# A streaming encoder layer on one core: where a head gain is multiplied, and the order of three short stages

## The chip, the cores and the metric

The kernel runs on one core of one Trainium2 chip. The metric is the device time of one execution in microseconds (us), given as the median of several runs. The engines are TensorE (PE, with its weight loads shown apart as PEld), VectorE (DVE), ScalarE (ACT), GpSimd (POOL) and SyncE (SP, which here only issues transfers). Each engine takes its instructions in a fixed order, and a waiting instruction holds all that stand behind it on its engine.

## The reference

One layer of a hybrid encoder, for 1024 new tokens and 32 tokens of a running stream (the decode tokens). All of it is in f32.

```python
def mixer(xn, ...):                       # xn = rms_norm(x, g_mix_pre)
    proj = xn @ w_in                      # split into q, k, v, gates of three head groups
    o_a = head_rms_norm(gla(...), g_a) * silu(gr)
    o_b = head_rms_norm(hgrn2(...), g_b) * silu(hg)
    o_c = head_rms_norm(mlstm(...), g_c) * sigmoid(mo)
    cat = concatenate([o_a, o_b, o_c], axis=-1)
    return cat @ w_out                    # g_a, g_b, g_c together are g_head, one number per column of cat

x = x + rms_norm(mixer(...), g_mix_post)
up = causal_dwconv(rms_norm(x, g_ffn_pre) @ w_up)
gate, val = split(up)
x = x + rms_norm((gelu(gate) * val) @ w_down, g_ffn_post)
```

`head_rms_norm(x, g)` divides each head by its root mean square and multiplies by g. So g_head is one factor per column of `cat`, and may as well be one factor per row of `w_out`.

## The kernel before, in words

**Arithmetic.** Most products are made from two halves of each f32 operand: a high half rounded by a cast (`xh`, `woh`, ...) and a low half, the difference (`xl`, `wol`, ...). A product is then three matmuls, high by high, low by high and high by low (`mm3`, lines 87 to 90), which accumulate in one bank of PSUM. `split` (line 92) makes the halves: ACT casts, DVE subtracts.

**Stages.** The tokens are cut into three groups (384, 384, and 256 with the 32 decode tokens). For each group the input projection runs (`inproj`): first the token-major v columns and gates (`vg`, tiles `pv`, one block `blk` of 256 columns after another, one tile for every 128 tokens), then the feature-major q, k and forget columns (tiles `pf`). The third group makes its v and gate blocks feature-major and turns them back (`vg_across`, tiles `pv`, `vf`, `pb`). The work of the mixer in units of 128 tokens (units 0 to 7, and 8 for the decode tokens; `mixer`) is interleaved with the projections of the following groups, until some 487 us. Then the output projection of the units follows (`outproj`; the first is `RING[0]`, unit 0), interleaved with the mixers of units 6 and 7, until some 641 us. The seam to the up-projection runs from there to some 675 us, then the up-projection `up_all` until after 1200 us, and `down_all` to the end. The up-projection forms each 2 x 2 block of products by seven products p1 to p7 of sums of blocks (`PROD`; operands A.. and S.. of the weights, B.. and T.. of the tokens), and `s` is 0 or 1 for the two halves of 256 tokens that the first step takes apart.

**What sets the order.** The program writes generators that hand over to each other with `yield`, and a scheduler orders the instructions of every engine by their priorities and its own estimates; `tc.high_priority` moves instructions forward, `tc.issue_after` keeps them behind a given one. So a small edit can move instructions far from it. Tiles come from pools; a tag with `bufs=n` has n places in turn, and who writes a place waits for the readers of the tile that lay there before.

**The places that matter here:**
- Gates. `vg_store` takes a bank `pv` or `pb`. Blocks 4 to 7 are gates: ACT makes a tanh into `vth` (or `gth` in the third group), DVE completes it (L432, L434), POOL multiplies by `gh`, the broadcast half of g_head, into `vg` (L436), and POOL issues the write to the DRAM tensor `g_d` (L437). The mixer reads it back as `gt` and multiplies it into `cat`.
- Keys. `keys` transposes a unit's four key blocks on PE into the bank `mi`, two at a time. ACT copies both halves of each pair into `kt2` (64 x 256, L888); the second pair goes into the same bank.
- First out-projection unit. `out_weights` makes `woh` and `wol` from the raw tiles `wor`, six of which are loaded early. The ring of 128 x 1024 tiles has `NRING` = 7 places, and `CT0` = 6 raw tiles lie ahead of the first `ct` tile; the last two raw tiles follow later. `outproj` transposes `cat` (tiles `ct`, `ctp`, halves `ch`, `cl`) and makes for every k both halves of the columns, three matmuls each. `om` and `cat` of the decode unit, 8, stand among them.
- Seam. `up_block` for f = 0 and s = 0, 1, with the operands of f = 1 being made meanwhile by `up_operands`, and the T2 and T4 operands copied on ACT (L2047).

## Time and profile before

| | |
|---|---|
| median of 3 runs | 1328.7 us (1328.49 to 1329.58) |
| profiled execution | 1326.9 us, its span 1325.1 us, mean granted PE clock 0.992 |
| PE busy | 1290.7 us, 97% of the span |
| DVE busy | 1008.1 us, 76% |
| ACT busy | 700.0 us, 53% |
| POOL busy | 286.1 us, 22% |
| chain of work that ended last | PE 73%, DVE 14%, DMA 4%, ACT 4%, issue 3%, POOL 2% |

The span is the time between the first and the last instruction in the profile; 1.8 us of the execution lie around it. A row of a timeline has the start in us from the span's beginning, the duration of the row, engine, line, operation, output and inputs, shapes, and the number of instructions that it joins; in brackets stands the idle time of the engine before it and what ended it. Tile names are written without numbers, so `kt` is the program's `kt2`, and `q` or `fr` stand for tiles of any group. Matmuls overlap, so a row's duration is not its share of PE's time. The granted clock of PE is 1.00 at full rate.

### The profile page before, as it was taken

What the parts mean: (1) busy time and instruction counts of PE and PEld (TensorE: products, weight loads), DVE (VectorE), ACT (ScalarE), POOL (GpSimd) and SP (SyncE); (2) the same over time, 40 slices, a digit from 0 to 9 for tenths busy, and PEclk for the clock granted to TensorE, in tenths of its full rate; (3) what the DMA queues carried; (4) which work ended last, traced back from release to release, by engine and by line L of the source; (5) the groups of instructions that cost most, each with busy time, mean ns of one, the idle gap of its engine ahead of it and who ended that gap; (6) DMA issues with size and microseconds to landing.
All of it is one profiled execution on the core that took longest, in us unless ns stands there. A gap on an engine that the chain in (4) does not pass through costs nothing.

```text
span 1325.1 us, 25585 instructions
## 1 busy us (share of the span) xinstructions
PE 1290.7 (97%) x9896; PEld 1095.0 (83%) x9896; DVE 1008.1 (76%) x1761; ACT 700.0 (53%) x1298; POOL 286.1 (22%) x390
## 2 busy tenths in 40 slices
PE   6999999999989999999999999999999999999997
PEld 6999889998889987868887777778888887778885
DVE  5795639778698778786997777778888876499556
ACT  5655556555575555445864545445455454454552
POOL 4532403145122263223100101111111000020005
PEclk9999999999999989999999999999999999999999
DMA  9799778886889954634439988855574349845425
GB/s 340 244 356 372 263 254 253 301 275 198 301 277 306 348 173 151 192 110 150 132 147 306 299 245 246 243 154 152 136 182 129 100 148 353 327 141 152 136 88 127
DMA packets 134784, 291.73 MB, mean 220 GB/s; under 512 B 29015, under 2 KB 63991, under 8 KB 132535
## 3 DMA queue, kind: packets, MB, share of 16 engines
q1 hardware_dynamic: 119831, 262.71, 58.4%
q0 software_dynamic: 10320, 22.94, 8.7%
q10 hardware_dynamic: 4512, 4.46, 1.0%
q8 instruction: 77, 1.26, 0.4%
q14 instruction: 44, 0.36, 0.1%
HBM read 229.38 MB, written 85.78 MB: 238 GB/s over the span
## 4 chain that ended last, share of the span: by engine, by line
PE 73%; DVE 14%; DMA 4%; ACT 4%; issue 3%; POOL 2%; SPq 0%; DVEq 0%; POOLq 0%; ACTq 0%
PE pux_None L88 4%; PE pux_None L90 4%; PE pux_None L89 4%; PE puw_None L90 3%; PE puw_None L88 3%; PE puw_None L89 3%; PE q L88 3%; PE q L90 3%; PE q L89 3%; PE pv L88 3%; PE pv L89 2%; PE pv L90 2%; PE x L88 2%; PE x L89 2%; PE x L90 2%
## 5 line engine op out<-in xcount | busy, mean ns | idle before, releaser
L1453 DVE SCALAR_TENSOR_TENSOR y<-uu,fconv_sb,y 128x1024 f32<-128x1024 f32 x88 | 112.9, 1283 | 21.8 <-ACT y L1451 20.1
L1450 POOL COPY fhalo<-uu 128x2 f32<-128x2 f32 x44 | 18.3, 416 | 382.5 <-DVE uu L1363 382.5
L1451 ACT ACTIVATE y<-uu,fconv_sb 128x1024 f32<-128x1024 f32 x44 | 54.8, 1245 | 5.6 <-DVE uu L1363 5.1
L88 PE MATMUL pv<-wt_0h,xh_all 128*128 128x256 f32 (+1 forms) x192 | 56.1, 292 | 0.9 <-DVE xl_all L326 0.7
L89 PE MATMUL zp<-wol,ch 128*128 128x512 f32 (+1 forms) x144 | 57.0, 396 | 0.0
L88 PE MATMUL zp<-woh,ch 128*128 128x512 f32 (+1 forms) x144 | 57.0, 405 | 0.0
L90 PE MATMUL zp<-woh,cl 128*128 128x512 f32 (+1 forms) x144 | 56.6, 394 | 0.0
L90 PE MATMUL pv<-wt_0h,xl_all 128*128 128x256 f32 (+1 forms) x192 | 54.7, 285 | 0.0
L89 PE MATMUL pv<-wt_0l,xh_all 128*128 128x256 f32 (+1 forms) x192 | 54.6, 284 | 0.0
L88 PE MATMUL pv<-wt_1h,xh_all 128*128 128x256 f32 (+1 forms) x192 | 54.3, 283 | 0.0
L89 PE MATMUL pv<-wt_1l,xh_all 128*128 128x256 f32 (+1 forms) x192 | 54.3, 283 | 0.0
L90 PE MATMUL pv<-wt_1h,xl_all 128*128 128x256 f32 (+1 forms) x192 | 54.3, 283 | 0.0
L211 POOL TENSOR_SCALAR gss<-gss 128x1 f32<-128x1 f32 (+1 forms) x9 | 13.0, 1442 | 175.2 <-ACT gjk L1722 175.1
L206 POOL TENSOR_SCALAR hrs<-hss 128x5 f32<-128x5 f32 (+3 forms) x27 | 10.7, 396 | 171.1 <-DVE hss L1011 166.5
L827 DVE COPY_PREDICATED P<-masks_sb,sc 128x352 f32<-128x352 int32 (+3 forms) x53 | 38.0, 716 | 7.9 <-PE sc L738 7.3
L88 PEld LDWEIGHTS pv<-wt_0h,xh_all 128*128 128x128 f32 x192 | 36.4, 190 | 2.2 <-DVE xl_all L326 1.1
L1011 DVE TENSOR_REDUCE hss<-sq 128x5 f32<-128x320 f32 (+3 forms) x27 | 13.6, 504 | 30.9 <-ACT sq L1010 30.8
L89 PEld LDWEIGHTS pv<-wt_0l,xh_all 128*128 128x128 f32 x192 | 36.4, 190 | 0.1
L90 PEld LDWEIGHTS pv<-wt_0h,xl_all 128*128 128x128 f32 x192 | 36.4, 189 | 0.1
L207 POOL TENSOR_TENSOR hrs<-hrs,mhalf 128x5 f32<-128x5 f32 (+3 forms) x27 | 35.9, 1329 | 2.2
L88 PEld LDWEIGHTS pv<-wt_1h,xh_all 128*128 128x128 f32 x192 | 36.0, 187 | 0.3 <-issue 0.2
L89 PEld LDWEIGHTS pv<-wt_1l,xh_all 128*128 128x128 f32 x192 | 35.9, 187 | 0.1
(1900 smaller groups left out, 4632.4 us busy)
## 6 DMA issues: line engine op xcount, KB each, us to landing
wus<-in_w_us SPq DMA_DIRECT2D x16, 1024.0 KB, 10.1
wrP<-in_w_dn SPq DMA_DIRECT2D x27, 512.0 KB, 8.5
ht<-h_d SPq DMA_DIRECT2D x22, 512.0 KB, 8.3
wt_0r<-in_w_tok SPq DMA_DIRECT2D x21, 512.0 KB, 3.8
wt_1r<-in_w_tok SPq DMA_DIRECT2D x21, 512.0 KB, 7.3
h_d<-y SPq DMA_DIRECT2D x21, 512.0 KB, 2.6
ws_d<-in_w_dn POOLq DMA_DIRECT2D x20, 512.0 KB, 7.8
wrP<-ws_d SPq DMA_DIRECT2D x20, 512.0 KB, 6.2
```

The costliest lines, as they stand in the source:

```text
L88: pe.matmul(ps, lh[0], rh[0], start=first, stop=False, **kw)
L89: pe.matmul(ps, lh[0], rh[1], start=False, stop=False, **kw)
L90: return pe.matmul(ps, lh[1], rh[0], start=False, stop=last, **kw)
L206: pool.tensor_scalar(out, ss, 1.0 / width, eps, op0=ALU.mult, op1=ALU.add)
L207: pool.tensor_tensor(out, out, mhalf[:n, :cols], op=ALU.pow)
L211: pool.tensor_scalar(out, m0, m1, EPS, op0=ALU.add, op1=ALU.add)
L827: dve.copy_predicated(dst, mk.broadcast_to([n, 11, *mk.shape[2:]]), src)
L1011: dve.tensor_reduce(ss[:n, h0:h0 + nh], sq3, axis=mybir.AxisListType.X, op=ALU.add)
L1450: behind["POOL"] = pool.tensor_copy(fhalo[:, j, :], u[:, SEQ - 2:SEQ])
L1451: act.activation(y, u, AF.Identity, scale=fconv[:, j, 2:3], bias=fconv[:, j, 3:4])
L1453: dve.scalar_tensor_tensor(y, uu[i][:, s:s + SEQ], fconv[:, j, s:s + 1], y, op0=ALU.mult, op1=ALU.add)
```

## The change

- **g_head.** POOL's product L436, the tile `gh`, its load and its scaling go. `gcols` gets eight columns more, g_head by rows of `w_out` (`ghead`, halved once on DVE). `out_weights` multiplies: the high half is an ACT activation with `ghead` as its scale, the low half a DVE scalar_tensor_tensor (raw times `ghead`, less the high half). The tanh goes straight into the tile that is written to `g_d`; the tag `vg` has four places instead of three, and `vth` is gone. In the third group the tile written to `g_d` is the `gth` tile itself.
- **Keys.** All four transposes go into the bank in one visit, and ACT then makes two copies of 64 x 512 instead of four of 64 x 256.
- **First out-projection unit.** `NRING` is 10 and `CT0` 8, so that all raw tiles are loaded ahead of the first `ct`. The unit first makes the products with the high weights for all k (four matmuls for each k), then those with the low weights. All low halves are kept behind `halves[1]`, the `cl` of the unit.
- **vf.** The copies of `vf` are issued at high priority.
- **Seam.** p7 of f = 0, s = 0 is kept behind the latest product; the A12 operand of f = 1 is made a step earlier, and the copies of T4 stand behind it; p3 of s = 1 stands behind p4.

The core of the diff:

```diff
         def vg_store(blk, u, off, n, ps):
-            o = mx.tile([128, 256], F32, tag="vg", name=f"vg{u}_{blk}", bufs=3)
             t = t0 + off
+            o = gate[0].tile([128, 256], F32, tag="gth", name=f"gth{u}_{blk}", bufs=3) if gate and blk > 3 else \
+                mx.tile([128, 256], F32, tag="vg", name=f"vg{u}_{blk}", bufs=4)
...
-            ia = tanh(th[:n], ps[:n, :256], 0.5)
+            ia = tanh(o[:n], ps[:n, :256], 0.5)
...
-            pool.tensor_tensor(o[:n], th[:n], gh[:n, c0:c0 + 256], op=ALU.mult)
             pool.dma_start(g_d[t:t + n, c0:c0 + 256], o[:n])
...
-                    act.copy(fs[e], ps)
+                    with tc.high_priority(offset=AHEAD):
+                        act.copy(fs[e], ps)
...
-    NRING, CT0 = 7, 6
+    NRING, CT0 = 10, 8
...
         def keys():
-            for f0 in (0, 2):
-                kps = small(2, 128)
-                for f in (f0, f0 + 1):
-                    soon(pe.transpose, kps[:n, f - f0, :], khf[:, f * n:f * n + n], ident)
-                for ch, (o, m) in enumerate(chunks):
-                    with tc.high_priority(offset=AHEAD):
-                        act.copy(kt2[o:o + m, ch, 128 * f0:128 * f0 + 256], kps[o:o + m].rearrange("p f n -> p (f n)"))
+            kps = mi.rearrange("p a b -> p (a b)").rearrange("p (f n) -> p f n", n=128)
+            for f in range(4):
+                soon(pe.transpose, kps[:n, f, :], khf[:, f * n:f * n + n], ident)
+            for ch, (o, m) in enumerate(chunks):
+                with tc.high_priority(offset=AHEAD):
+                    act.copy(kt2[o:o + m, ch, :], kps[o:o + m].rearrange("p f n -> p (f n)"))
...
     def out_weights(W):
         for k in range(8):
-            if k < 2:
-                split(W[1][k], W[2][k], wo_raw[k], dve)
-            else:
-
-                with tc.issue_after(halves[0].ins):
-                    act.copy(W[1][k], wo_raw[k])
-                with tc.issue_after(halves[1].ins):
-                    dve.tensor_tensor(W[2][k], wo_raw[k], W[1][k].bitcast(F32), op=ALU.subtract)
+            with tc.issue_after(halves[0].ins) if k > 1 else ExitStack():
+                act.activation(W[1][k], wo_raw[k], AF.Copy, scale=ghead[:, k:k + 1])
+            with tc.issue_after(halves[1].ins):
+                dve.scalar_tensor_tensor(W[2][k], wo_raw[k], ghead[:, k:k + 1], W[1][k].bitcast(F32), op0=ALU.mult,
+                                         op1=ALU.subtract)
             yield
...
                 next(W[3])
+                for x in range(2):
+                    for hf in range(2):
+                        pe.matmul(pss[hf][:n], chs[k][x], woh[k][:, cs[hf]], start=k + x == 0, stop=False,
+                                  skip_group_check=True)
+            for k in range(8):
                 for hf in range(2):
-                    product(pss[hf], hf, k)
+                    pe.matmul(pss[hf][:n], chs[k][0], wol[k][:, cs[hf]], start=False, stop=k == 7, skip_group_check=True)
...
         def prod(ps, p, first, last):
-            product(ps, p, W, X, first, last, at)
+            with tc.issue_after(ends[-1]) if f == 0 and p == "p7" else ExitStack():
+                product(ps, p, W, X, first, last, at)
...
-            with tc.issue_after(kept["B11"].ins):
-                for n in ("T2", "T4"):
+            for n, ins in (("T2", "B11"), ("T4", "A12")):
+                with tc.issue_after(kept[ins].ins):
                     for t, e in zip(X[n], early[n]):
                         act.copy(t[:, :, :256], e)
```

Where the scheduler puts things now is read from the order of the instructions of the two programs. The numbers behind names tell tiles apart and differ between the programs.

PE at the keys of unit 4 (`mi<-ident,kh` are the transposes of its keys, `rows` a small stage of the third group's gates, `pf_10` and `pf_11` two feature blocks of the projection). Before, the second pair stands between them:

```order
L90 MATMUL pf_10_5380<-xh_all,wf_10l 128x288
L629 MATMUL rows_5433<-r_dc_5010,cf_sb 128x5 x3
L631 MATMUL rows_5433<-ident,r_st_4999 128x128 x2
L631 MATMUL rows_5433<-ident,r_st_4999 32x128
L738 MATMUL mi<-ident,kh_5161 128x128 x2
L88 MATMUL pf_11_5451<-xh_all,wf_11h 128x288
```
Now all four transposes stand ahead of `pf_10`, and here is:

```order
L90 MATMUL pf_10_5320<-xh_all,wf_10l 128x288
L627 MATMUL rows_5373<-r_dc_4952,cf_sb 128x5 x3
L629 MATMUL rows_5373<-ident,r_st_4941 128x128 x2
L629 MATMUL rows_5373<-ident,r_st_4941 32x128
L88 MATMUL pf_11_5391<-xh_all,wf_11h 128x288
```
The key transposes are gone from behind `rows`, and `pf_11` follows at once.

DVE at the same place (`q<-th,pf_1` empties the bank that `pf_11` needs; `Qz`, `Ld` and `x` belong to unit 4's scores, `e` and `fr` to the third group's forget gates). Before:

```order
L861 TENSOR_TENSOR Qz_152<-x_2_5493,qe_5305 128x128 x2
L549 TENSOR_TENSOR e_4703<-e_4703 128x288
L847 TENSOR_TENSOR x_8_5660<-b_5137 128x512
L852 TENSOR_TENSOR Ld_150<-x_2_5493,k_5136 128x128x2
L857 TENSOR_TENSOR Qz_152<-x_2_5493,q_5135 128x128
L548 TENSOR_SCALAR fr_4702<-fr_4702,oml 128x288
L553 SCALAR_TENSOR_TENSOR e_4703<-cf_sb,e_4703 128x288
L567 SCALAR_TENSOR_TENSOR q_5285<-th_5287,pf_1_5260 64x288
```
Now:

```order
L854 TENSOR_TENSOR Qz_153<-x_2_5433,qe_5247 128x128
L565 SCALAR_TENSOR_TENSOR q_5227<-th_5229,pf_1_5202 64x288
L542 SCALAR_TENSOR_TENSOR e_4645<-fr_4644,e_4645 128x288
L854 TENSOR_TENSOR Qz_153<-x_2_5433,qe_5247 128x128
L547 TENSOR_TENSOR e_4645<-e_4645 128x288
L845 TENSOR_TENSOR Ld_151<-x_2_5433,k_5078 128x128x2
L850 TENSOR_TENSOR Qz_153<-x_2_5433,q_5077 128x128
L840 TENSOR_TENSOR x_8_5600<-b_5079 128x512
```
q has moved ahead of one Qz and of the rows e, Ld, Qz and x, which now follow it.

DVE at the first out-projection unit (`wol` is the last low half, `cl` the low half of the next unit's transposed `cat`, `cat` the decode unit's own, which reads the bank `og` that PE's `om` takes next). Before:

```order
L1073 TENSOR_TENSOR wol_6902<-wor_6871,woh_6894 128x1024
L942 TENSOR_TENSOR C_0_7760<-C_1_6507,dcs_5434 128x195
L804 TENSOR_TENSOR kh_7404<-b_7349 128x512
L847 TENSOR_TENSOR x_32_7420<-b_7349 128x512
L1011 TENSOR_REDUCE hss_7052<-sq_6_7273 32x5
L792 COPY dec_7396<-eb_7394 128x8
L798 TENSOR_TENSOR qz<-q_7347,eb_7394 32x2x128 x2
L798 TENSOR_TENSOR qz<-q_7347,eb_7394 32x128 x2
L798 TENSOR_TENSOR qz<-q_7347,eb_7394 64x256
L798 TENSOR_TENSOR qz<-q_7347,eb_7394 64x384
L1102 TENSOR_TENSOR cl_7040<-ctp_7034,ch_7039 128x512
L1013 TENSOR_TENSOR cat_7051<-og_7201,hrs_7053 32x384
```
Now, from the rows behind that low half on, and again at its end:

```order
L1091 TENSOR_TENSOR cl_6954<-ctp_6948,ch_6953 128x512
L1003 TENSOR_REDUCE hss_6966<-sq_0_7179 32x6
L935 TENSOR_TENSOR C_0_7143<-C_0_7143,mi 128x130
L936 TENSOR_TENSOR C_0_7143<-C_0_7143,mi 64x65
L797 TENSOR_TENSOR kh_7317<-b_7262 128x512
```
```order
L791 TENSOR_TENSOR qz<-q_7260,eb_7307 64x384
L800 TENSOR_TENSOR kh_7317<-kh_7317,k_7261 128x512
L1005 TENSOR_TENSOR cat_6965<-og_7114,hrs_6967 32x384
L934 TENSOR_TENSOR C_0_7671<-C_1_6447,dcs_5374 128x195
L845 TENSOR_TENSOR Ld_151<-x_32_7333,k_7261 128x8x32
```
`cl` has moved to the front, directly behind the low halves; the C product (`C<-C,dcs`) has moved behind `cat`, and the product of `kh` with k ahead of it.

More of the change, by code (lines that the diff above doesn't have):

```diff
@@ L239, in small @@
         return t if len(shape) == 1 else t.rearrange("p (a b) -> p a b", b=shape[1])
-    gh = p1.tile([128, 1024], F32, name="gh")
     cols_of, dcs_of, behind = {}, {}, {}
@@ L493, in vg_across @@
             load_cat(0)
-            for k in range(CT0, 8):
-                wo_raw.append(ring[0](f"wor{k}"))
-                raw_out(k)
         tgs = pf.tile([128, 3, 26], F32, tag="tgs", name=f"tgs{g}")
@@ L1309, in up_operands @@
         yield res
-        with tc.high_priority(offset=AHEAD) if f == 1 else ExitStack():
-            for name, src in (("A12", a12), ("A11", a11)):
+        for name, src in (("A12", a12), ("A11", a11)):
+            with tc.high_priority(offset=AHEAD) if f == 1 else ExitStack():
                 res[name] = weight_halves(f"{name}_{f}h", src)
+            if f == 1 and name == "A12":
+                yield
         with tc.issue_after(kept["T2l"].ins) if f == 1 else ExitStack():
@@ L1432, in up_block @@
             prod(z, "p4", True, True)
+            if s:
+                with tc.issue_after(ends[-1]):
+                    prod(w, "p3", False, True)
         out(0, 1, c6, w)
@@ L1541, in up_all @@
                     next(late, None)
+                    if f == 0:
+                        ops = up_operands(1, raw.pop(1))
+                        W[1] = next(ops)
+                        next(ops)
+                        yield
                     m = (2 * f + (1 if s is None else s) - 3) * len(SUMS) // 34
@@ L1554, in up_all @@
                 if s != 0 and f + 1 < NF:
-                    ops = up_operands(f + 1, raw.pop(f + 1))
-                    W[f + 1] = next(ops)
+                    if f:
+                        ops = up_operands(f + 1, raw.pop(f + 1))
+                        W[f + 1] = next(ops)
                     for _ in ops:
@@ L2048, in body @@
             for x, c in zip(last, (slice(0, 128), slice(128, 256))):
-                with tc.issue_after(done[0].ins), tc.issue_after(kept["c6"].ins):
+                with tc.issue_after(kept["first"].ins), tc.issue_after(kept["c6"].ins):
                     next(x)
```

28 lines of the change are left out of this document (15 added, 13 removed).

## The prediction

> **What bounds the kernel now.** I read the busy times of the page first, then TensorE's (PE's) waits, then stretches cut around the longest of them.
>
> ```profile
> PE 1290.7 (97%) x9896; PEld 1095.0 (83%) x9896; DVE 1008.1 (76%) x1761; ACT 700.0 (53%) x1298; POOL 286.1 (22%) x390
> ```
> ```profile
> PE xt L322 <- DVE x L302: 9.6, 1, 9.6
> PE mi L738 <- ACT kt L888: 5.2, 2, 3.1
> ```
> ```profile
> PE pv L88 <- ACT vf L486: 1.5, 3, 1.2
> PE oi L738 <- DVE cat L1013: 1.1, 1, 1.1
> ```
> PE is busy 1290.7 of 1325.1 us, so 34.4 us are idle (a wait's columns: us in total, times, longest). The first 9.6 us are the start, which the change leaves alone, as it does the end. It can win only among the small waits between, and in what the clock does after them. The columns of the next rows are the length, the busy time of PE, PEld, DVE, ACT and POOL, then PE's granted clock:
>
> ```profile
> 139.60:145.50 5.90, 3.21 (x98) 2.45 (x98) 5.76 (x17) 4.41 (x12) 1.67 (x3) 1.00 0.64 235
> 145.50:148.90 3.40, 3.40 (x23) 2.95 (x24) 3.18 (x9) 1.98 (x6) 2.13 (x3) 0.50 0.51 143
> 391.20:394.70 3.50, 0.40 (x3) 0.20 (x2) 3.47 (x11) 3.15 (x9) 0.00 (x0) 1.00 1.07 360
> 394.70:398.10 3.40, 3.09 (x13) 3.04 (x13) 3.34 (x8) 3.34 (x12) 0.58 (x2) 0.50 0.95 296
> 656.90:660.90 4.00, 1.79 (x6) 0.89 (x6) 4.00 (x8) 3.86 (x9) 0.00 (x0) 1.00 0.00 0
> 660.90:664.30 3.40, 3.40 (x9) 2.63 (x8) 3.40 (x6) 0.00 (x0) 0.00 (x0) 0.51 0.00 0
> 700.00:750.00 50.00, 50.00 (x248) 37.28 (x241) 38.01 (x50) 22.23 (x33) 3.95 (x6) 1.00 0.93 296
> ```
> Three times a stretch in which PE idles 2.7, 3.1 and 2.2 us is followed by 3.4 us at a clock of 0.50. Half of 3.4 is 1.7 us of PE work lost each time, where PE is the bound. From 700 us on PE is busy 50.00 of 50 us: what is won before arrives at the end undiminished. But in the second and third pair DVE is busy 3.47 of 3.50 and 4.00 of 4.00 us. There PE's wait is the visible side of a full DVE.
>
> The Trainium skill (TensorE: Matmul & The Clock Gate, its table of what to keep to) asks for no idle gap over about 3 us between matmuls; by that, stretches with 2.2 to 2.7 us of idle would keep the clock. The rows show that they did not, so the trace decides, and I charge 1.7 us from about 2 us of idle on. By the skill's rule alone the sum below would be 2.6 us larger.
>
> **The change part by part.** *Keys of unit 0.* The second pair of transposes waits for the copies of the first pair, which lie in the same bank: one of the two waits for kt, 5.2 - 3.1 = 2.1 us.
>
> ```profile
> 141.37 0.66 PE L322 MATMUL xt<-ident,x 128*128 128x128 f32 x4 [0.38 <-DVE vth L432]
> ```
> ```profile
> 141.43 0.43 ACT L856 ACTIVATE x<-x 128x256 f32<-128x256 f32 x1
> ```
> ```profile
> 141.57 0.87 POOL L436 TENSOR_TENSOR vg<-vth,gh 128x256 f32<-128x256 f32 x1 [2.20 <-ACT x L850]
> ```
> ```profile
> 141.56 1.03 DVE L861 TENSOR_TENSOR Qz<-x,qe 128x128 f32<-128x128 f32 x2
> ```
> ```profile
> 142.72 0.48 DVE L861 TENSOR_TENSOR Qz<-x,qe 128x128 f32<-128x128 f32 x2
> ```
> Four transposes in one visit leave this wait no place, and the new order puts whole projections behind the keys. What goes: 5.90 - 3.21 = 2.69 us of idle, and 1.7 us of clock. What is late next: the first of these projections needs a bank that a tanh empties, and on ACT that tanh stands behind the exponential that now ends at 141.86. With a tanh of some 0.4 us (rows below) it ends near 142.3 to 142.5. Until then, from 139.6 on, PE has only eight transposes, 2 x 0.66 us: 2.8 - 1.3 = 1.5 us idle, in pieces. So 2.69 - 1.5 = 1.2 us are won if the clock still falls, 2.9 if it doesn't, 4.4 if no wait is left. I take **2.9**: the pieces are nearest to the single wait of 1.2 us for vf above, which no half clock follows.
>
> The gate product leaves POOL (36 of about 0.87 us). POOL is on no path here; but the two DVE products beside it took 1.03 us and the next two 0.48, so each costs DVE 0.55 us. The Trainium skill (SBUF — State Buffer, Who interferes with whom) says that a DVE instruction with two SBUF inputs and a GpSimd one that reads SBUF contend; the rows agree.
>
> *Keys of unit 4.* The longest wait inside, 3.1 us until 394.34:
>
> ```profile
> 381.27 0.45 DVE L577 SCALAR_TENSOR_TENSOR r_fm<-r_fm,e 5x288 f32<-5x288 f32 x1 [1.70 <-ACT e L537]
> ```
> ```profile
> 384.68 0.49 DVE L1011 TENSOR_REDUCE hss<-sq 128x5 f32<-128x320 f32 x1 [0.84 <-ACT sq L1010]
> ```
> ```profile
> 405.12 0.46 DVE L546 TENSOR_TENSOR fr<-e,fr 64x288 f32<-64x288 f32 x1
> ```
> ```profile
> 407.35 0.95 DVE L827 COPY_PREDICATED P<-masks_sb,sc 128x352 f32<-128x352 int32 x1
> ```
> ```profile
> 408.89 0.75 PE L738 MATMUL sc<-Qz,Ld 64*64 64x64 f32 x36
> ```
> The wait goes, and q, for which the next projection waits, moves forward on DVE. PE would stand before the score matmuls of 408.89 up to 3.1 + 1.7 = 4.8 us earlier, at 404.1. But these need the masked copy that DVE ends at 408.30, and ahead of that copy DVE has the same work as before except the 0.46 us of fr. It can be earlier by that and by the 0.84 us that it stood for a reduction (now further behind), 1.3 us together, and at best by the 1.70 us as well. So PE goes on at 407.0, at best at 405.3: 1.9 or 3.6 us won. The rest of the old wait comes back as up to 2.9 us (407.0 - 404.1) for DVE; with a half clock behind it, where PE is the bound, 0.2 us is left. I take **1.0**, about halfway from 0.2 to 1.9, as the new wait falls in two or three pieces. The other seven units' keys have no such wait and win nothing.
>
> *First out-projection unit.* All raw weights are there early, the high halves go first, the low halves follow:
>
> ```profile
> 502.01 1.23 DVE L1073 TENSOR_TENSOR wol<-wor,woh 128x1024 fp32r<-128x1024 f32 x1 [0.50 <-ACT woh L1071]
> 504.94 0.36 DVE L942 TENSOR_TENSOR C<-C,dcs 128x195 f32<-128x195 f32 x1 [1.71 <-DMA out_q_c<-C]
> ```
> ```profile
> 509.96 0.53 DVE L1013 TENSOR_TENSOR cat<-og,hrs 32x384 f32<-32x384 f32 x1
> 510.43 0.67 DVE L807 TENSOR_TENSOR kh<-kh,k 128x512 f32<-128x512 f32 x1
> ```
> ```profile
> L1190 ACT ACTIVATE z<-xr,oss x8: 1136/1151/1156, 523.3 to 651.2; 128x1024 f32<-128x1024 f32 x8
> ```
> ```profile
> L1073 DVE TENSOR_TENSOR wol<-wor,woh x6: 1209/1218/1227, 495.0 to 502.0; 128x1024 fp32r<-128x1024 f32 x6
> ```
> ```profile
> L311 DVE SCALAR_TENSOR_TENSOR x<-x,rs,gx x8: 1273/1285/1759, 12.0 to 307.8; 128x1024 f32<-128x1024 f32 x7, 32x1024 f32<-32x1024 f32 x1
> ```
> A scaled high half costs ACT 1.15 us, a low half DVE 1.29 instead of 1.22: eight times 0.07 are 0.5 us. PE's products would end some 4 us earlier. Yet behind the transposes of the next unit stands the decode unit's om, and it waits for this cat. Ahead of cat DVE loses the waits of 1.71 (the C product moves behind) and 0.50 us and the C product itself, 0.36; it gains kh, 0.67, and the 0.5. So cat ends 1.71 + 0.50 + 0.36 - 0.67 - 0.5 = 1.4 us earlier, and PE waits for it about as much longer as its products end sooner than that, some 2.6 us. Ends: 1.4, and with a half clock behind that wait -0.3. I take **-0.3**, as all three long idles above were followed by one.
>
> *Casts of vf.* Put at high priority, but in ACT's order vf still stands behind squares that wait for DVE:
>
> ```profile
> 472.14 0.47 ACT L1010 ACTIVATE sq<-hn 128x320 f32<-128x320 f32 x1 [1.20 <-DVE hn L1041]
> ```
> Ends 0 and 1.2; **0.3**, for a DVE with no POOL products beside it. For the same reason the 1.1 us of oi, among the second group's gates: **0.4**, ends 0 and 1.1.
>
> *Seam.* p7 moves behind p2, the A12 cast ahead of the T4 copies. PE's 2.2 us at 656.9 go or move, but DVE is full:
>
> ```profile
> 651.00:675.00 24.00, 21.79 (x140) 19.28 (x139) 23.50 (x34) 17.84 (x27) 0.77 (x2) 0.93 0.17 9
> ```
> ```profile
> 667.33 1.22 DVE L1262 TENSOR_TENSOR T4l<-xg,T4h 128x1024 fp32r<-128x1024 f32 x1
> ```
> ```profile
> 670.09 0.28 PE L89 MATMUL puz<-T4l,A_0h 128*128 128x256 f32 x1
> ```
> DVE ends T4l at 668.55 behind the same work as before; PE uses it at 670.09. More than these 1.5 us can't be won. Ends -0.2 (less a half clock of 1.7) and 1.5; I take **1.0**, near the upper end, as the present half clock lies ahead of this point and is paid already.
>
> The rest (the gh load, its scaling, the merged key copies, the scaling of ghead) stands where PE waits for nothing: 0.
>
> Sum: 2.9 + 1.0 - 0.3 + 0.3 + 0.4 + 1.0 = 5.3 us. Lower ends: 1.2 + 0.2 - 0.3 + 0 + 0 - 0.2 = 0.9; upper: 4.4 + 3.6 + 1.4 + 1.2 + 1.1 + 1.5 = 13.2. The profiled execution took 1326.9 us (span 1325.1); the median, 1328.7, lies 1.8 above it. So 1321.6 on the profiled execution, **1323.4** on the median.
>
> **The rivals.** *Waits only change their name.* DVE is full at two of the three places, and each moved wait of 2 us brings its half clock. Then the lower ends hold: 0.9 us, 1327.8, no change. For it: 3.47 of 3.50 and 23.50 of 24.00. Against it: unit 0, where no later step of DVE holds PE.
>
> *The idle goes and the clock stays up.* Upper ends of the four large terms: 4.4 + 3.6 + 1.4 + 1.5 = 10.9, 1317.8. For it: DVE gets rid of POOL's products. Against it: the DVE counts above. The skill's clock rule points this way.
>
> *Slower: gate tiles are held until their write has landed.* POOL's product used to free a gate tile for the next tanh; now its write to DRAM does, and the first scaled high half waits for such a write too, as its memory lies over a gate tile.
>
> ```profile
> DMA to landing us min/median/max: 1.8/4.5/8.5
> ```
> ```profile
> g_d<-vg POOLq DMA_DIRECT2D x6, 128.0 KB, 2.6
> ```
> ```profile
> 480.49 0.38 ACT L98 ACTIVATE gth<-pb 128x256 f32<-128x256 f32 x1
> ```
> ```profile
> 486.51 0.89 ACT L98 ACTIVATE gth<-pb 128x256 f32<-128x256 f32 x3
> ```
> ```profile
> 488.77 0.58 POOL L437 DMA_DIRECT2D g_d<-vg  x1 [0.30 <-POOL vg L436]
> ```
> ```profile
> 492.69 2.36 DVE L94 TENSOR_TENSOR wol<-wor,woh 128x1024 fp32r<-128x1024 f32 x2
> ```
> The first row is of all 36 writes, the second of those from 470 to 496 us. A block of gates comes every 6.0 us at the least; less tanh, gate step (0.4 each) and issue (0.6) a landing may take 4.6. With 7 us three blocks wait 2.4 us each, 7.2, and the low halves start at 488.8 + 7 + 1.15 = 496.95 instead of 492.69, cat with them 4.3 later: 11.5 against 5.3 gives 1328.7 + 6.2 = 1334.9. It turns the sign from 5.5 us on (3 x 0.9 + 2.7 = 5.4). The 2.6 us of the second row speak against it, the 8.5 of the first for it.
>
> **How the numbers follow.** The forecast (2.7 to 8 us won) gets 0.50, the idle gone 0.18, names only 0.22, slower 0.10. A measurement of this kernel can tell some 0.2%, 2.7 us, from no change. Faster by more: 0.50 + 0.18 = 0.68; same 0.22; slower 0.10. The range goes from 1316, just beyond the fast rival's 1317.8 and short of the 1315.5 of all upper ends, to 1329, just beyond names only; it leaves out the slower case and the best of the fast one.
>
> **What would show it.** Right: no PE wait for kt; PE waits for a masked copy of DVE near 405 and for cat near 506; DVE's T4l ready within 0.5 us of PE's use; PE busy 50.00 of 50 from 700 us on. Wrong: tanh or the first woh waiting over 3 us for a write of g_d (slower), or a granted clock of 1.00 from 139 to 700 us (faster). If om does not wait for cat, the third step is wrong.

## The result and the profile after

The changed kernel takes 1341.7 us (median of 4 runs, 1340.7 to 1342.5) beside 1329.1 for the kernel before: a ratio of 1.0087, 95% interval 1.0063 to 1.0111. It is slower by some 12 us; forecast were 5.3 us less. Its profiled execution has a span of 1340.7 us. Two executions of e10 and one of e11 below took 1587, 4191 and 2550 us, and the times given for these two leave them out.

The page's first row and then PE's waits (total, times, longest, in us):

```profile
PE 1299.1 (97%) x9896; PEld 1097.4 (82%) x9896; DVE 1004.7 (75%) x1761; ACT 699.1 (52%) x1281; POOL 267.6 (20%) x354
```
```profile
PE xt L322 <- DVE x L302: 9.8, 1, 9.8
PE sc L731 <- DVE P L820: 7.6, 3, 6.7
PE zp L1125 <- ACT woh L1059: 2.3, 1, 2.3
PE rows L627 <- ACT r_dc L609: 2.0, 1, 2.0
PE pf L88 <- DVE q L565: 1.7, 3, 1.0
PE pux_None L90 <- DVE A_1h L94: 1.7, 1, 1.7
PE pf L88 <- ACT q L672: 1.0, 1, 1.0
```

No wait for `kt` is left. New are one of 6.7 us for the masked copy `P`, one of 2.3 us for `woh`, one of 2.0 us for `r_dc`, and two of 1 us for `q` early on. But PE is busy 8.4 us longer than before (1299.1 against 1290.7), so waits are not all of it. To place the loss I count, in two traces, the PE instructions that both programs have, and take the difference of the times at which the same count is finished. Each column is the kernel's lead (-) or lag (+) in us on the kernel before, where that one stands at the time at the head of the column:

| at us | 60 | 140 | 200 | 480 | 560 | 600 | 640 | 700 | 1200 |
|---|---|---|---|---|---|---|---|---|---|
| after | -0.1 | +5.1 | -0.1 | -1.9 | -0.2 | +10.7 | +11.3 | +10.5 | +15.6 |
| e2, before, one side moved 32 bytes | -0.3 | -0.3 | +1.2 | +1.3 | +0.9 | +0.9 | +0.9 | -0.2 | +4.8 |
| e3, keys in one visit up to unit 5 | -0.4 | +4.5 | -0.6 | -2.0 | +1.6 | +2.0 | +4.2 | +3.4 | +8.5 |
| e5, after, both sides alike | -0.3 | +4.0 | -1.2 | -2.4 | +0.2 | +10.1 | +10.7 | +9.6 | +9.6 |
| e7, e5 with gate tiles in vg | -0.2 | +3.9 | -1.3 | -3.3 | -3.5 | -2.5 | -0.3 | -1.4 | -1.4 |
| e9, before with the keys alone | -0.2 | -0.2 | +0.8 | +3.7 | +5.1 | +15.3 | +15.9 | +15.3 | +15.3 |
| e12, before with the seam alone | -0.1 | -0.1 | +1.7 | +2.2 | +1.5 | +1.5 | +1.5 | +0.4 | +0.4 |
| e13, before with g_head alone | -0.2 | +4.4 | -0.6 | -1.0 | -1.5 | -0.4 | +1.9 | +2.5 | +2.5 |

One trace each: until 480 us e2 and e12 have the order of the kernel before, and yet lag by 1.3 and 2.2 us there, so a difference of 1 or 2 us between two kernels is not to be read. What the changed kernel loses until 140 us it has back by 200. Then it loses three times: 1.7 us from 480 to 560, 10.9 us from 560 to 600, and 5.1 us from 700 to 1200, where PE never waits.

**Unit 7.** PE's timeline around the wait, first of the kernel before, then of the changed one:

```profile
578.38 0.60 PE L1097 MATMUL ctp<-ident,ct 128*128 128x128 f32 x4
...
582.55 0.48 PE L88 MATMUL zp<-woh,ch 128*128 128x512 f32 x1
...
587.86 0.39 PE L90 MATMUL zp<-woh,cl 128*128 128x512 f32 x1
588.09 0.60 PE L1097 MATMUL ctp<-ident,ct 128*128 128x128 f32 x4
588.88 1.14 PE L738 MATMUL sc<-Qz,Ld 64*64 64x64 f32 x64 [0.19 <-DVE P L827]
```
```profile
581.37 0.66 PE L1086 MATMUL ctp<-ident,ct 128*128 128x128 f32 x4
581.86 1.04 PE L1201 MATMUL fxt<-ident,z 128*128 128x128 f32 x8
589.57 1.94 PE L731 MATMUL sc<-Qz,Ld 64*64 64x64 f32 x64 [6.67 <-DVE P L820]
591.43 1.88 PE L731 MATMUL sc<-cf_sb,x 128*128 128x11 f32 x8
593.24 2.91 PE L731 MATMUL mi<-v,kt 128*32 128x64 f32 x44
596.08 0.80 PE L88 MATMUL zp<-woh,ch 128*128 128x512 f32 x1
```

PE does the same scores at almost the same time (588.88 and 589.57), behind the same DVE chain. What changed is what it does meanwhile: before, 24 products `zp` of the next out-projection unit (unit 4; 582.55 to 588.1) fill the time; now they stand behind the scores and start at 596.08. These products need the second `cl` of their unit. On DVE it moved from ahead of the masked copy to behind it; the kernel before and after:

```profile
580.30 0.68 DVE L1102 TENSOR_TENSOR cl<-ctp,ch 128x512 fp32r<-128x512 f32 x1
...
587.90 0.93 DVE L827 COPY_PREDICATED P<-masks_sb,sc 128x352 f32<-128x352 int32 x1
```
```profile
588.49 0.93 DVE L820 COPY_PREDICATED P<-masks_sb,sc 128x352 f32<-128x352 int32 x1
589.22 0.71 DVE L1091 TENSOR_TENSOR cl<-ctp,ch 128x512 fp32r<-128x512 f32 x1
```

Traced further back, the transposes `ctp` ahead of this `cl` take a bank that ACT's copy of the decode unit's `z` empties, and that copy came later; before and after:

```profile
573.55 0.56 ACT L1127 COPY z<-zp 32x512 f32<-32x512 f32 x1
```
```profile
578.49 0.56 ACT L1116 COPY z<-zp 32x512 f32<-32x512 f32 x1
```

So far this is reading; what the experiments bear out is the place of the 24 products, not this chain behind it. A half clock follows the wait. The stretches of the changed kernel (columns as in the prediction):

```profile
582.90:589.57 6.67, 0.00 (x1) 0.03 (x1) 6.62 (x14) 1.15 (x2) 1.42 (x4) 0.73 0.62 177
589.57:599.30 9.73, 9.73 (x124) 8.39 (x125) 5.48 (x10) 0.00 (x0) 0.00 (x0) 0.50 0.28 73
```

6.67 - 0.19 us of idle and half of 9.73 make 11.3; from 560 to 620 the table's method gives 11.5 (-0.2 to +11.3).

**First out-projection unit.** ACT's first scaled high half, with the wait ahead of it:

```profile
492.41 8.43 ACT L1059 ACTIVATE woh<-wor,gcols_sb 128x1024 fp32r<-128x1024 f32 x8 [3.02 <-DMA g_d<-gth]
```

It waits 3.02 us for a gate tile's write to `g_d` to land: `woh` of k = 0 is placed over the `gth` tile of unit 7, and that tile is now read by the write itself. In the kernel before, the `gth` tiles lay clear of `woh`. It is the ring that moved them there: its three more places are 12 KB, and the `gth` tiles lie 12 KB further. By these places two parts of the change make the wait together. The new ring alone was not tried; e13, with g_head and the old ring, starts its first scaled halves without a wait:

```profile
486.30 2.17 ACT L1060 ACTIVATE woh<-wor,gcols_sb 128x1024 fp32r<-128x1024 f32 x2
```

**Up-projection.** The stretch 850 to 1000 us of the kernel before, then of the changed one:

```profile
850.00:1000.00 150.00, 150.00 (x676) 120.48 (x675) 124.63 (x161) 73.80 (x110) 18.39 (x27) 1.00 0.63 163
```
```profile
850.00:1000.00 150.00, 150.00 (x667) 118.89 (x666) 120.70 (x155) 75.07 (x112) 21.16 (x30) 1.00 0.61 165
```

Both have PE busy 150.00 of 150 us at a clock of 1.00, but 676 matmuls against 667. The first and the last of twelve matmuls in a row with T4, before and after:

```profile
911.51 0.39 PE L88 MATMUL puz_None<-T4h,A_12h 128*128 128x512 f32 x1
...
914.00 0.39 PE L90 MATMUL puz_None<-T4h,A_12h 128*128 128x512 f32 x1
```
```profile
904.50 0.40 PE L88 MATMUL puz_None<-T4h,A_11h 128*128 128x512 f32 x1
...
907.07 0.40 PE L90 MATMUL puz_None<-T4h,A_11h 128*128 128x512 f32 x1
```

Eleven steps take 2.49 us before, 226 ns each, and 2.57 us after, 234 ns.

### The profile page after: what moved, and what is told of

It reads as the page before. It is cut to its first block, busy times and chain, and to the rows that moved or that the text cites. A ratio compares the mean times of both kernels' runs of the same rounds, so it can differ in the third digit from the quotient of the medians.

```text
span 1340.7 us, 25537 instructions
## 1 busy us (share of the span) xinstructions
PE 1299.1 (97%) x9896; PEld 1097.4 (82%) x9896; DVE 1004.7 (75%) x1761; ACT 699.1 (52%) x1281; POOL 267.6 (20%) x354
## 4 chain that ended last, share of the span: by engine, by line
PE 78%; DVE 10%; DMA 5%; ACT 4%; issue 2%; POOL 1%; SPq 0%; DVEq 0%; POOLq 0%; ACTq 0%
PE pux_None L88 4%; PE pux_None L89 4%; PE pux_None L90 4%; PE pv L88 3%; PE pv L89 3%; PE pv L90 3%; PE puw_None L88 3%; PE puw_None L89 3%; PE puw_None L90 3%; PE q L88 3%; PE q L90 3%; PE q L89 3%; PE sc L731 3%; PE x L88 2%; PE x L90 2%; PE x L89 2%
## 5 line engine op out<-in xcount | busy, mean ns | idle before, releaser
L88 PE MATMUL zp<-woh,ch 128*128 128x512 f32 (+1 forms) x128 | 52.2, 408 | 0.3 <-DVE cl L1091 0.3
L89 PE MATMUL zp<-wol,ch 128*128 128x512 f32 (+1 forms) x128 | 51.0, 399 | 0.0
L90 PE MATMUL zp<-woh,cl 128*128 128x512 f32 (+1 forms) x128 | 50.5, 396 | 0.0
L1007 POOL TENSOR_TENSOR cat<-cat,gt 128x320 f32<-128x320 f32 (+3 forms) x27 | 34.6, 1283 | 24.4 <-DVE cat L1005 24.3
L731 PE MATMUL sc<-Qz,Ld 64*64 64x32 f32 (+5 forms) x1344 | 30.3, 220 | 7.9 <-DVE P L820 7.6
L731 PEld LDWEIGHTS sc<-Qz,Ld 64*64 64x64 f32 (+2 forms) x1344 | 25.1, 132 | 14.9 <-issue 12.8
```

The lines of the kernel that those rows point to most:

```text
L88: pe.matmul(ps, lh[0], rh[0], start=first, stop=False, **kw)
L89: pe.matmul(ps, lh[0], rh[1], start=False, stop=False, **kw)
L90: return pe.matmul(ps, lh[1], rh[0], start=False, stop=last, **kw)
L731: line[0] = fn(*args, **kw)
L1007: pool.tensor_tensor(cat[:n, c0:c0 + 64 * nh], cat[:n, c0:c0 + 64 * nh], gt[:n, c0:c0 + 64 * nh], op=ALU.mult)
```

## The experiments

Theories: the up-projection's loss comes from the **places** of its operands, rival: from new order and traffic. Unit 7's loss comes from the **order** of PE's queue, rival: DVE became late by itself. The wait for `woh` comes from the **landing** of the gate write. "Before" was 1327.6 to 1328.6 us in these comparisons.

**Places: e1, e2, e5.** `gcols` grew by 32 bytes in every partition, and with it the weights, B and T1, which lie behind it, moved by 32 bytes. T2, T3 and T4 lie on the other side of the memory and stayed. In the kernel before, all of these tiles start at multiples of 256 bytes.

```diff
-    gcols = const("gcols_sb", [128, 16], F32, a["gcols"])                              # after
+    gcols = const("gcols_sb", [128, 24], F32); sp.dma_start(gcols[:, :16], a["gcols"])  # e1
-    gcols = const("gcols_sb", [128, 8], F32, a["gcols"])                               # before
+    gcols = const("gcols_sb", [128, 16], F32); sp.dma_start(gcols[:, :8], a["gcols"])   # e2
-    p7.tile([128, 40], F32, name="pad1")                                               # after
+    p7.tile([128, 32], F32, name="pad1")                                               # e5
```

> The changed kernel, but with gcols 24 columns wide (16 loaded) instead of 16, so that the tiles behind it lie 64 bytes further than in the kernel before and not 32; the order of every engine is the same. Address theory (the up-projection lost 5 us because its left-side operands now stand 32 bytes off a multiple of 64 and T2, T3 and T4 do not): PE's spacing in the up-projection returns to 227 ns for all operands and the time falls by some 5 us to 1336.7. Rival, the new order of the seam and of the third-group tiles brings more SBUF traffic beside the matmuls: no change, 1341.7. Under both, unit 7's wait of 6.7 us stays.

> The kernel before, but with gcols 16 columns wide (8 loaded), so that the tiles behind it lie 32 bytes further, as in the changed kernel; nothing else differs, and the order of every engine is the same. Address theory: the time rises by some 5 us, to 1334, with 230 to 235 ns between the matmuls that take T2, T3 and T4. Rival, order and traffic: no change, 1329.

> The changed kernel, with the pad tile behind the tokens' operands cut from 40 to 32 columns (160 to 128 bytes). That moves T2, T3 and T4 up by the same 32 bytes by which gcols moved the weights, B and T1; the order of every engine is the same as in the changed kernel. Two runs have shown that a move of one side alone by 32 or by 64 bytes costs 5 us in the up-projection. Theory, the two sides must stand alike (in the kernel before all of them were multiples of 256 bytes): spacing 227 ns again, 5 us less, 1336.7. Rival, the left side must stand where it stood: no change, 1341.7. Unit 7's wait of 6.7 us and the 2.3 us for woh stay under both.

Measured: e1 1341.3, no gain (ratio to before 1.0094, interval 1.0074 to 1.0113). e2 1334.5, slower by 1.0042 (1.0026 to 1.0059) with the order untouched. e5 1335.8 (1.0058, 1.0045 to 1.0071); against the ratios of e1 and of the changed kernel, 1.0094 and 1.0087, that is 4 to 5 us less. The stretch of e1, e2 and e5:

```profile
850.00:1000.00 150.00, 150.00 (x667) 118.69 (x667) 121.39 (x155) 74.69 (x112) 21.74 (x30) 1.00 0.61 164
```
```profile
850.00:1000.00 150.00, 150.00 (x666) 118.81 (x666) 122.73 (x158) 72.27 (x110) 18.70 (x27) 1.00 0.63 163
```
```profile
850.00:1000.00 150.00, 150.00 (x676) 120.44 (x675) 123.10 (x158) 75.24 (x113) 21.20 (x30) 1.00 0.63 167
```

So my first form of the theory, a multiple of 64 bytes, fell with e1. What fits all of these runs: the two operands of a matmul must lie alike; a move of one side by 32 or 64 bytes costs 5 us, the same move of both costs nothing. The pads move other tiles too, so that it is the matmul's own two operands rests on which matmuls slow down most: those with T2, T3 and T4, by 4 to 7 ns each. The rival fell with e2.

**Order in unit 7: e3, e4, e9.** Two visits as before for the units named, one visit for the rest; e3 and e4 stand on e1 (so with the 5 us of misplacement), e9 on the kernel before.

```diff
-        def keys():                # one visit, all units
+        if u < 6:                  # e3; in e4 no unit
+            def keys():            # one visit
...
+        else:
+            def keys():            # two visits
...
```

> As e1_pad64, but the keys of units 6, 7 and 8 go in two visits as in the kernel before (units 0 to 5 in one visit). In its order the 24 products zp of the next out-projection unit stand ahead of unit 7's last scores again. Order theory (the wait of 6.7 us and the half clock behind it come from these 24 products standing behind the scores): PE waits there for less than 1.5 us, no half clock from 582 to 600 us, and the time falls by some 11 us against e1_pad64, to 1326. Rival, VectorE became late by itself (it waits for the halves on ScalarE and for GpSimd): the masked copy P ends as late, against the same work on PE a wait of 5 us or more stays, and the time is 1333 or more.

> As e1_pad64, but the keys of all units go in two visits as in the kernel before. Order theory: no wait of 6.7 us in unit 7, some 11 us less than e1_pad64, and more than e3_keys_lt6 by what the one visit wins in units 0 to 5: by the prediction's terms for units 0 and 4, 3.9 us, so 1330; if those terms were won nowhere, the same as e3_keys_lt6, 1326. Rival, VectorE late by itself: a wait of 5 us or more in unit 7, 1333 or more.

> The kernel before with the keys in one visit, nothing else. In its order too the 24 products zp stand behind unit 7's last scores. Order theory: a wait of 5 to 7 us in unit 7 and its half clock, 11 us, less what the one visit wins in units 0 and 4 (3.9 us by the prediction, 0 at the least): 1336 to 1340. Rival, unit 7's wait needs the other parts of the change too: 1325 to 1329.

Measured: e3 1335.6 (1.0050, 1.0032 to 1.0068), e4 1338.5 (1.0074, 1.0056 to 1.0093), e9 1342.4 (1.0111, 1.0098 to 1.0124). Unit 7's last scores in e3 and e9:

```profile
589.96 1.14 PE L731 MATMUL sc<-Qz,Ld 64*64 64x64 f32 x64
```
```profile
594.80 1.93 PE L738 MATMUL sc<-Qz,Ld 64*64 64x64 f32 x64 [6.70 <-DVE P L827]
```

In e3 the wait is gone and 560 to 600 us costs 0.4 us instead of 10.9. Yet the time fell by 5.7 us and not by 11. e1 stood at -4.2, -2.9, +7.9 and +8.5 at 480, 560, 600 and 640 us. From 480 to 560 e3 loses 3.6 us where e1 lost 1.3 (the half clock at 490 us lasts 10.2 us in e3 and 6.8 in e1), and after 600 us 2.2 where e1 lost 0.6. The lead of 4.2 us that e1 had at 480 is 2.3 more than the changed kernel has there in the same order, so it tells nothing of e3's order, and where the rest of the missing 5 us goes stays open. e4, with the old keys, has no wait at these scores either, but loses 8.8 us from 560 to 640 in smaller waits (for `cl` 1.9 and 1.1 us); that expectation missed. e9 is the strong one: the keys in one visit alone make the kernel before nearly 15 us slower, 10.2 of them at the same place.

**Landing: e7, e8.** Both on e5. In e7 the third group's gate tiles are `vg` tiles, so no write lies under `woh`; e8 has the old keys too.

```diff
-            o = gate[0].tile([128, 256], F32, tag="gth", name=f"gth{u}_{blk}", bufs=3) if gate and blk > 3 else \
-                mx.tile([128, 256], F32, tag="vg", name=f"vg{u}_{blk}", bufs=4)
+            o = mx.tile([128, 256], F32, tag="vg", name=f"vg{u}_{blk}", bufs=4)
```

> As e5_same_residue, but the gate tiles of the third group are vg tiles like those of the first two (in the changed kernel they lie where woh comes to lie). All keys go in one visit. In its order the 24 products zp stand ahead of unit 7's last scores. Landing theory (the first scaled high half waits for the last gate write to land): ScalarE's wait for g_d goes and with it PE's 2.3 us for woh and the half clock behind it, 3 us. Order theory for unit 7: its wait of 6.7 us and the half clock go, 11 us. Together 1336.7 - 3 - 11 = 1322.7. Rival, VectorE late by itself in unit 7: 1333. Rival, a wait for another cause takes the place of the one for woh (the cl halves end only at 491): 1325.5.

> As e7_gates_vg, but with the keys of all units in two visits as before. Its order has the 24 products zp behind unit 7's last scores again, as the changed kernel has, though the keys are the old ones. Order theory: PE waits 5 to 7 us there, half a clock behind it, and the time is 11 us above e7_gates_vg, 1333.7, plus 0 to 3.9 us for what the one visit wins in units 0 and 4. Rival, the one visit of the keys is itself what hurts in unit 7 (ScalarE's copies of 64 x 512 hold the halves up): no wait, 1322.7 to 1326.6.

Measured: e7 1327.5, level with the kernel before (0.9999, 0.9989 to 1.0010); e8 1330.0 (1.0018, 1.0006 to 1.0031). ACT's first scaled halves in e7, and unit 7's last scores in e7 and e8:

```profile
484.35 2.17 ACT L1059 ACTIVATE woh<-wor,gcols_sb 128x1024 fp32r<-128x1024 f32 x2
```
```profile
585.47 1.14 PE L731 MATMUL sc<-Qz,Ld 64*64 64x64 f32 x64 [0.75 <-DVE P L820]
```
```profile
584.02 1.94 PE L731 MATMUL sc<-Qz,Ld 64*64 64x64 f32 x64 [2.44 <-DVE P L820]
```

Both waits went in e7, with all keys in one visit: the one visit does no harm in unit 7 by itself. e8 has the old keys and the products behind the scores, and the wait again, though of 2.4 us and not 5 to 7, as the masked copy is done at 584.0 there. In all kernels here, 24 products or more ahead of the scores went with 0 to 0.75 us of wait (before, e2, e3, e4, e7, e10 to e13, e15), products behind them with 6.66 to 6.71 (after, e1, e5, e9, e14) or 2.44 (e8). The order theory holds, its rival doesn't. It is the scheduler that sets the order, and edits far away turn it.

**First unit: e10, e14.** e7 leads by 6.7 us at 505 us and by 3.6 at 520: PE waits 2.2 us for a bank that ACT's copy of `z` empties. Both stand on e7 and make the low products half by half; e14 also forces that order.

```diff
-            for k in range(8):
-                for hf in range(2):
+            for hf in range(2):
+                for k in range(8):    # e14: the second half issued after the first, copies at high priority
                     pe.matmul(pss[hf][:n], chs[k][0], wol[k][:, cs[hf]], start=False, stop=k == 7, skip_group_check=True)
+                leave(pss[hf], hf)
```

> As e7_gates_vg, but the first out-projection unit makes its low products half by half (all eight k of the first 512 columns, then of the second), and each half is copied out as soon as it is done. In e7_gates_vg both halves end with the last two products, and PE then waits 2.2 us for a bank that ScalarE's copy of z empties. Theory, the bank is late because both halves end together: ScalarE begins some 1.8 us earlier, the wait falls to 0.4 us or less and the half clock behind it goes: 1327.5 - 1.8 - 1.7 = 1324. Rival, ScalarE's copy stands behind other work that is late (the exponential of kh, which waits for VectorE): the wait stays over 1.5 us, 1327.5.

> As e7_gates_vg, but the low products of the first out-projection unit's second half are kept behind the last of the first half, and the copies out are at high priority. Its order has the 24 products zp behind unit 7's last scores again, as the changed kernel has. If the wait of 2.2 us at 503 us comes from both halves ending together: PE waits there for 0.5 us or less, no half clock behind it, and at 520 us the kernel is some 6 us ahead of the one before instead of 3.6. Rival, ScalarE is late with the copy for other work: 1.5 us or more stay. Under both, unit 7 then costs it a wait of 5 to 7 us and its half clock, 10 us: 1327.5 - 2.5 + 10 = 1335, or 1337.5 under the rival.

Measured: e10 1326.1 (0.9984, 0.9972 to 0.9996), the 2.2 us unchanged, since the scheduler still let both halves alternate. e14 1333.7 (1.0038, 1.0024 to 1.0053): the wait for `z` is gone, one of 1.27 us for the next unit's `cl` stands in its place, and at 520 us it leads by 3.4 us and not by 6. From 480 to 560 us it won 1.9 us where e7 won 0.2: the theory is right on the wait, but most of what it frees goes to the next one. Unit 7 cost e14 10.6 us, as its order said.

**Parts: e11, e12, e13, e15.** e11: e10 with only units 0 and 4 in one visit. e12: the kernel before with the seam's part alone. e13: with g_head alone, the pad cut as in e5. e15: with g_head and seam, gate tiles as in e7.

> As e10_low_by_half, but only units 0 and 4 have their keys in one visit, the others in two. Its order has 41 of the products zp ahead of unit 7's last scores. If the one visit wins only in units 0 and 4 and costs where it moves the order of the others (as the kernel before with the keys in one visit alone suggests, which lost 2 us near 330 and 2 near 490 us): no wait over 1 us in unit 7, and 1 to 3 us less than e10_low_by_half, 1321 to 1323. Rival, the other units' keys win as well: 1 to 3 us more, 1325 to 1327.

> The kernel before with only the seam's part of the change (p7 behind the latest product, A12 a step earlier with the T4 copies behind it, p3 of s = 1 behind p4). By the prediction's step: the wait of 1.6 us for A_1h near 657 us goes or moves, 1.0 us less, 1326.6; by the progress of the two traces between 640 and 680 us, 1 to 1.6 us less. Rival, VectorE is full and the wait only changes its name: no change, 1327.6.

> The kernel before with only the g_head part of the change, and the pad tile cut so that both sides of the up-projection stand alike. The first two low halves are not kept behind halves, as before; keys, order of the first unit, vf and seam are the old ones. Landing theory: the first scaled high half waits for the last gate write, and the first out-projection unit ends up to 3 us later. What POOL's products leave free is worth what the changed kernel had won at 480 us where the keys did not win it, 0 to 2.4 us: 1328.2 to 1330.6. Rival, the first unit's high halves were not on the path in the old order (PE had the decode unit's products there): 1325.2 to 1327.6.

> The kernel before with g_head and the seam alone, gate tiles of the third group in vg, pad tile cut to 32 columns; keys, order of the first unit and casts of vf as before. Its order has 24 products zp ahead of unit 7's last scores. If the parts add: the kernel before with g_head alone stood 1.1 us below the kernel before, that with the seam alone 1.2, and the first scaled high half no longer waits for a write of a gate, 0 to 0.6: 2.3 to 2.9 us below the kernel before, a ratio of 0.998. Rival, the parts move each other's order: no change or slower, a ratio of 1.000 or more.

Measured: e11 1333.5 (1.0036, 1.0023 to 1.0049), a miss: unit 7's scores wait for nothing, but PE waits 2.4 us for `cat` and 1.4 for `P` between 549 and 562 us. e12 1327.4 (0.9993, 0.9982 to 1.0004), 1.1 us won at the seam by the table, but not told apart from no change by its time. e13 1327.4 (0.9991, 0.9980 to 1.0001), not told apart either; the wait for a gate's write that was expected of it did not come. e15 1326.3 (0.9984, 0.9974 to 0.9995): what the two parts would give together, though its interval does not part it from either alone. With e10 it is the best version here, some 2 us below the kernel before.

## Why the prediction was wrong, point by point

- **"From 700 us on PE is busy 50.00 of 50 us: what is won before arrives at the end undiminished", and "The rest ... stands where PE waits for nothing: 0".** Two steps that failed together. The sum had no term for the eight more columns of `gcols`, and their 32 bytes slowed the matmuls: 5.0 us (e2, e5). A full busy share says that PE never waits, not that its matmuls keep their pace; the count in the same row does.
- **"The other seven units' keys have no such wait and win nothing."** True of the wait, but the step priced nothing for the order that the edit turns. It cost 10.9 us in unit 7 (e9 alone 10.2). I looked for places where the change works and not for places where PE has cover that can move: 24 products that filled 5.5 us.
- **Keys of unit 0, +2.9.** The wait for `kt` went, and by 200 us the kernel had won 5.1 us back, more than I gave it. But e13, with the old keys, wins the same 5.0, and e9, with the new keys alone, keeps a wait of 2.5 us there and wins nothing. It was g_head's reordering that did it. That part also lost ahead of it, between 60 and 140 us, what I had at 0: PE is idle 2.8 us there, waits of 1.0 us each for two `q` among them, and the table's 5.1 holds besides what the new order only puts later. Net at 200 us: 0.1 to 1.3 us won.

The two waits in the changed kernel's timeline of PE; e13 has them too (1.02 and 0.98), e9 and e12 don't:

```profile
64.06 0.44 PE L88 MATMUL pf<-xh_all,wf_1h 128*128 128x384 f32 x1 [1.02 <-ACT q L672]
...
69.56 0.44 PE L88 MATMUL pf<-xh_all,wf_10h 128*128 128x384 f32 x1 [0.99 <-DVE q L565]
```

The trace shows where the second `q` lost a part of its time. A DVE product took 0.55 us in the kernel before and takes 2.76 in the changed one, as a product of POOL now lies ahead of it; an ACT step waits 1.88 us for it, and the tanh for this `q` stands behind that step. The prediction had read such a lengthening beside POOL's gate products, and counted it only where it goes. Why g_head's part brings the two products together was not tried. Before, and then after:

```profile
62.41 0.55 DVE L613 TENSOR_TENSOR r_ig<-r_ig,r_bb 5x384 f32<-5x384 f32 x1
```
```profile
63.70 2.78 POOL L94 TENSOR_TENSOR wf_10l<-wf_10r,wf_10h 128x1024 fp32r<-128x1024 f32 x1 [2.52 <-ACT wf_10h L93]
64.13 2.76 DVE L611 TENSOR_TENSOR r_ig<-r_ig,r_bb 5x384 f32<-5x384 f32 x1
```

- **Keys of unit 4, +1.0.** The old wait of 3.1 us became one of 1.98 us, but for ACT's `r_dc` and not for DVE's masked copy, with its half clock; from 380 to 420 us 0.3 us were won. That does not bear the step out. e4 and e8, with the old keys, won 0.6 and 0 there by the same count, and e13, with the old keys, has the wait for `r_dc` too (1.92 us). e9, with the new keys alone, waits 4.29 us for `q` and loses 0.9: that `q` moves forward on DVE was read from the order of the whole change, and the keys do not bring it about. The last two rows are e9's, at unit 0 and at unit 4.

```profile
391.26 1.29 PE L627 MATMUL rows<-r_dc,cf_sb 5*128 5x5 f32 x6 [1.98 <-ACT r_dc L609]
```
```profile
145.01 0.67 PE L738 MATMUL sc<-Qz,k 64*64 64x64 f32 x32 [2.51 <-issue]
...
398.21 0.61 PE L88 MATMUL pf<-xh_all,wf_11h 128*128 128x288 f32 x1 [4.29 <-DVE q L567]
```

- **First out-projection unit, -0.3.** Measured -1.7 from 480 to 560 us. The wait for `cat` came (0.57 us), but the larger one is the 2.33 us for `woh`. That was one half of my slower rival, its first scaled half held by a write. Its other half, gate tiles waiting in turn, came too: ACT's tanh stood 3.32 us (at 473.9 us) and 1.43 us for a gate's write, so both signs that I had named for it were there. But PE's waits beside them are 0.5 us or less, where I had charged 7.2 us of PE. I had given this rival 0.10, for the 2.6 us of the median landing. With the wait for `woh` out (e7) the step is worth some +0.2 (-3.3 to -3.5), within what one trace can tell of what I had.

```profile
482.49 0.38 ACT L98 ACTIVATE gth<-pb 32x256 f32<-32x256 f32 x1 [1.43 <-DMA g_d<-gth]
```

- **vf and oi, +0.7.** `oi` waits 0.8 instead of 1.1 us. Where PE waited 1.17 us for vf it now waits 0.48, for DVE's `Qz`. From 420 to 480 us the changed kernel won 0.9, which is less than two traces of one order can differ by, so the size is not shown.
- **Seam, +1.0.** From 640 to 700 us the changed kernel won 0.8, e12 1.1; the new wait of 1.65 us for `A_1h` draws no half clock. That looks right, but e2, with the seam's old order, won 1.1 there as well: in its trace the half clock behind the old wait is missing. So the size is that of a half clock that comes or not, and stays open.

The stretch behind the old wait in e2, where the prediction's row of the kernel before has 0.51:

```profile
661.00:664.00 3.00, 2.65 (x12) 2.12 (x12) 3.00 (x6) 0.62 (x2) 0.00 (x0) 1.00 0.00 0
```

- **The slower rival**, 1334.9, had the sign right and the smallest of the three causes.

## What to carry to other kernels

In a kernel whose order a scheduler makes, ask of an edit not only what it frees but which cover it may move: list the stretches where an engine's slack is filled by other work, and read in the new order, at each, whether that work still stands there. A table that grows by a few bytes moves every tile behind it; compare the start addresses of the operands that meet in matmuls before and after. And where a tile is now read by a transfer, look what is placed over it next, in the new layout and not the old one: that work waits for the landing.

## What the runs showed of the hardware

- Matmuls of 128 x 512 came every 226 to 227 ns where both operands lay alike, and every 233 to 234 ns (T2, T3, T4) where one side was moved by 32 or 64 bytes against the other, with PE busy throughout and a granted clock of 1.00. T2 is slower from the start, 229 ns before. T1 and B21, which lie on the same side as the weights, kept their pace. B11 and B22 lie there too and yet went from 226.7 to 228 or 229 ns (e1, e2 and the changed kernel); they stand behind T3 and T2 in PE's order, and e5 restored them. Why they lose is open. The Trainium skill (SBUF — State Buffer, Operand start alignment) asks only for a start at a multiple of the element size and says that its runs timed nothing; the runs here show that more matters for the pace. Which multiple decides (128, 256 or another) stays open.
- The half clock came in whole pieces of 3.4 us: by the clock that the traces hold, each stretch between the start and the end lasted 3.4, 6.8, 10.2 or 13.7 us, in all kernels here. How many pieces does not follow from the wait. Waits of 6.66 to 6.71 us drew 13.7 us (after, e1, e14; it begins within the wait) or 10.2 (e5, e9), and e8's of 2.44 us drew 10.2 (584 to 594 us, the first and the last full stretch below). One order drew different numbers: at 145 us the kernel before had 3.4 us, e2 and e12 6.8, and at the seam it came in one trace and not in another. That alone puts two traces of the same order 1.7 us apart.
- The prediction's three half clocks were not all of the kernel before. A fourth, of 6.8 us, stands at 490 us behind a stretch in which PE was busy 6.14 of 6.30 us and waited for nothing longer than 0.16 us, so a wait of 2 us is not needed for one; e7 has none there. The charge of 1.7 us for each wait is one piece, the least that was seen; in unit 7 it was 4.9.

```profile
484.00:490.30 6.30, 6.14 (x114) 4.78 (x113) 4.47 (x18) 5.63 (x15) 3.90 (x7) 1.00 0.68 168
490.30:497.10 6.80, 6.80 (x49) 5.59 (x47) 6.61 (x12) 5.44 (x7) 1.52 (x3) 0.50 0.85 312
```

The stretches of e8:

```profile
584.00:586.00 2.00, 1.98 (x65) 1.94 (x65) 1.93 (x6) 0.00 (x0) 0.00 (x0) 0.50 0.89 352
...
592.00:594.00 2.00, 2.00 (x7) 1.54 (x6) 1.80 (x4) 0.00 (x0) 0.00 (x0) 0.52 0.11 33
```
